# Convolution taps laid between the score groups, and weight splits taken out of the attention, in a two-layer hybrid decoder trunk

## The chip, the cores and the metric

The kernel runs on one core of a Trainium2 chip. The metric is the device time of one execution, in microseconds; lower is better. Three executions of the kernel before took 1790.84, 1791.62 and 1792.38 us, so the median is 1791.62 us. Every change here moves work in time or between engines; what is computed stays the same.

The engines are named as the profile names them: PE is TensorE (PEld its weight loads), DVE is VectorE, ACT is ScalarE, POOL is GpSimd and SP is SyncE, which only issues DMAs here.

## The reference

Two layers run over 512 tokens of width 1024, all in float32:

```python
for l in range(2):
    h = x + 0.5 * swiglu(rms_norm(x), w1, w3, w2)            # FFN 1, inner width 2816
    p = rms_norm(h) @ w_in                                   # 2*384 conv, 384 q, 128 k, 128 v, 256 q_mem
    y_conv = silu(layer_norm(depthwise_conv31(a * sigmoid(gate)) + b))   # 384 channels, causal, 31 taps
    y_swa  = sliding_window_attention(q, k, v, sinks)        # 6 heads of 64, window 128, blocks of 128
    y_mem  = memory_attention(q_mem, mk, mv)                 # 4 heads of 64, 256 memory tokens
    h = h + concat(y_conv, y_swa, y_mem) @ w_out
    h = h + 0.5 * swiglu(rms_norm(h), w1b, w3b, w2b)         # FFN 2
    x = rms_norm(h)
```

Queries and keys are normalised by head and the window's ones rotated. The softmax of the window has a learned sink for each head, whose exponential is added to the denominator.

## The kernel before

**Products.** A float32 product is made of three: each operand is split into a high and a low part (hi is rounded, lo is the rest), and `mm3` (L176 to L178) adds hi·hi, lo·hi and hi·lo. A split is one ACT copy for hi (L145 or L150) and either a DVE subtraction for lo (L146), or, for some weights, a second ACT copy with the sign turned (L151) and an accumulating DMA issued by POOL (L152) that adds the weight to it. Activations are split with their gain by L155 (ACT, `xhi`) and L156 (DVE, `xlo`); L236 squares them for the norm (`sq`). The tiles `whi/wlo` and `ghi/glo` are all such pairs.

**Stages.** In each layer FFN 1 is followed by the mixer (from about 355 to 530 us in layer 0, and some 883 us later in layer 1), the out-projection and FFN 2. The mixer's steps are issued in the order of a string, `ORDER`: `c00` to `c21` are the halves of the convolution's input product for three chunks of 128 channels, `q0` to `q3` the query and key products of four token blocks with the weights wqk (`Q`: their transposes), `v0` to `v3` the value and memory-query products (`V`: transposes), `g0` and `g1` the first two groups of scores, `a` the attention, `t0` to `t2` the convolution's taps, one chunk each, and `s` the layer norm, swish and out-projection. A scheduler then places instructions of all engines by their dependences and its own clock; `tc.issue_after(x)` keeps what stands under it behind the instruction x.

**Attention.** Ten groups of scores (`GROUPS`) go one after another: memory attention (`r`) of blocks 0 and 1, window attention (`w`) of blocks 0, 1, 2, the rest of blocks 1 and 2, then `r` of blocks 2 and 3 and `w` of block 3 in two parts. A group is: scores on PE (L763 with the mask, L769), maxima on DVE (L773 or L788, two reductions), small DVE operations that make the bias (L774, or L789 and L790), the sink's term on POOL (L791, `esw`), exponentials on ACT (L800; `uu`, `pr`), transposes on PE (L810), a copy on ACT (L812, `aux`), and the product with the values on PE (L821, `po`). When a block is complete DVE makes the reciprocal of the denominator (`rd`, L830, L831 or L833) and scales (L835, `aux`), and PE transposes the result (L844, `pt`) for the out-projection. Scores run two groups ahead.

**Taps.** A tap is one DVE instruction over 512 tokens of a chunk of 128 channels (L939, `there`). There are 93 for each layer. The first `EARLY` = 49 may run as soon as their input is there; of the rest, `LATER[n]` are allowed once the bias of group n is made (1, 12, 5, 4, 3, 3, 3, 3, 3, and the last 7 behind the last group), and the scheduler puts them where it finds room, also between the two maxima of a group. When all are done POOL adds the three chunks (L945, L946) for the norm's mean, whose product on PE is L950.

**Splits in the mixer.** wqk has four weight tiles; the last three use the ACT copy and the POOL DMA (`glo<-in_wqk`). The eight weight tiles of the out-projection are split by `out_weights(d)`: d = 0 and 1 after the last key transpose, 2 and 3 inside the attention ahead of groups 3 and 5, the others in `s`. `kept(spread(r), "RL")` copies the layer norm's factor, by ACT. At the end of layer 0 the rescale of h for the next layer (eight DVE operations) runs in one piece inside FFN 1 of layer 1.

Of the kernel before, what the change touches and what calls it, by code (L numbers as in the profile page):

```python
# [13 lines left out]
AF = mybir.ActivationFunctionType  # L14
ALU = mybir.AluOpType
# [49 lines left out]
def trunk(ctx: ExitStack, tc: tile.TileContext, xT, memT, pos, w1a, w3a, w2a, w1b, w3b, w2b,  # L65
# [160 lines left out]
    class Stat:  # L226
# [5 lines left out]
        def square(self, out, src, scale):  # L232
            if self.on:
                self.on.tensor_tensor(out=out, in0=src, in1=src, op=ALU.mult)
            else:
                A.activation(out, src, AF.Square, scale=scale)  # L236

# [103 lines left out]
    def up_pair(l, w13, f, M):  # L341
# [26 lines left out]
        def add(out, a, b):  # L368
            V.tensor_tensor(out=out, in0=a, in1=b, op=ALU.add)  # L369

# [14 lines left out]
        for i in range(2):  # L385
            w = unit(X[i])
            product(xy[i][:, x0], w, 1, 5)
            A.activation(part[i][:, x0], xy[i][:, x0], AF.Copy)
            product(zv[i][:, x1], w, 0, 7)
            add(to[i][:, :, x1], zv[i].rearrange("p (n t) -> p n t", n=2), part[i][:, x0].unsqueeze(1).to_broadcast([P, 2, QT]))  # L390
        w = unit(z)
# [13 lines left out]
    def ffn(l, w13, w2, x, sums, factors, last, at_product, aside=None):  # L405
# [44 lines left out]
        for q, (f0, nf) in enumerate(QUARTERS):  # L450
            ahead = 2 if q + 1 < len(QUARTERS) else 0
            for f in range(f0, f0 + nf + ahead, 2):
                if f not in g:
                    g[f], g[f + 1] = up_pair(l, w13, f, M)
                    if f == PLAIN:
                        with tc.issue_after(M.gated.ins):
                            after()
            begun = []

            def begin(d):  # L460

                w = weights(w2[l, d, :, f0 * P : (f0 + nf) * P], nf * P, V)
                ps = bank([P, S], "mm")
                for j in range(nf - 2):
                    mm3(ps, at(w, ALL, blk(j)), g[f0 + j], j == 0, False)
                begun.append((ps, w))

            for d in range(KD):
                while len(begun) < (d + 1 if ahead or d else 3):
                    with nullcontext() if ahead or d else queued():  # L470
                        begin(len(begun))
                ps, w = begun[d]
                for j in range(nf - 2, nf):
                    mm3(ps, at(w, ALL, blk(j)), g[f0 + j], False, j == nf - 1)
                added = V.scalar_tensor_tensor(out=h[:, d, :], in0=ps, scalar=0.5, in1=h[:, d, :], op0=ALU.mult, op1=ALU.add)  # L475
                if not ahead:
                    last(d)
            if aside and not q:
                aside(added)
# [62 lines left out]
    def heads(x):  # L542
        return x.rearrange("p (h e) -> p h e", e=HD)

    def head_scale(ps, col, n, out=None):

        sq = tm("hsq", "sq", 2)[:, 0 : n * HD]
        A.activation(sq, ps, AF.Square, scale=col)
# [73 lines left out]

    def mixer(l, x, st, last):
        o = CC * TAPS
# [101 lines left out]
        def values(t):  # L726
# [23 lines left out]
        by_half = lambda z: z.rearrange("p (c i) -> p i c", i=2)  # L750
        sinks, nsinks = by_half(sink), by_half(nsink[:, l, :])

        def scored(kind, pairs):
# [17 lines left out]
            if not masked:  # L771
                for i in range(2):
                    V.tensor_reduce(out=nmr[:, b, i], in_=pp[i], axis=AX.X, op=ALU.max)  # L773
                biased[len(biased)] = V.scalar_tensor_tensor(out=nmr[:, b], in0=nmr[:, b], scalar=-1.0, in1=by_half(rm[:, b, :]),  # L774
                                                             op0=ALU.mult, op1=ALU.mult)
                return pp, W
# [5 lines left out]
            else:  # L782
# [3 lines left out]
                rr = by_half(rq[:, b, 0:NH])[:, :, c : c + n]  # L786
            for i in range(2):
                V.tensor_reduce(out=each(nmw, i), in_=pp[i], axis=AX.X, op=ALU.max)  # L788
            V.scalar_tensor_tensor(out=at_(nmw), in0=at_(nmw), scalar=-1.0, in1=rr, op0=ALU.mult, op1=ALU.mult)  # L789
            biased[len(biased)] = V.tensor_tensor(out=at_(nmw), in0=at_(nmw), in1=per(nsinks), op=ALU.min)  # L790
            G.tensor_tensor(out=at_(esw), in0=at_(nmw), in1=per(sinks), op=ALU.add)  # L791
# [31 lines left out]
        def scaled(kind, b, po):  # L823
# [3 lines left out]
            if kind == "w":  # L827
                e = esw[:, b]
                A.activation(e, e, AF.Exp)
                V.tensor_tensor(out=rd.rearrange("p (c i) -> p i c", i=2), in0=po[:, :, HD].rearrange("p (c i) -> p i c", i=2), in1=e, op=ALU.add)  # L830
                V.reciprocal(rd, rd)  # L831
            else:
                V.reciprocal(rd, po[:, :, HD])  # L833
# [27 lines left out]
        def attention():  # L861
# [17 lines left out]

            for d in range(2):  # L880
                with tc.issue_after(keyed[2].ins):
                    out_weights(d)
            yy.extend([gated_pair() for _ in range(KD // 2)][::-1])
            y.extend(at(p, ALL, i, ALL) for p in yy for i in range(2))
            for n, (kind, *pairs) in enumerate(GROUPS):
# [3 lines left out]
                if final:  # L889
# [40 lines left out]

        def taps(c):
            V.tensor_scalar(out=cv[:, c, :], in0=ypad[:, c, 0:S], scalar1=conv_w[:, c, 0:1], scalar2=conv_b[:, c : c + 1],
                            op0=ALU.mult, op1=ALU.add)
            for j in range(1, TAPS):

                n = c * TAPS + j - EARLY
                group = sum(n >= sum(LATER[:g]) for g in range(1, len(LATER)))
                with tc.issue_after(biased[group].ins) if n >= 0 else nullcontext():
                    V.scalar_tensor_tensor(out=cv[:, c, :], in0=ypad[:, c, j : j + S], scalar=conv_w[:, c, j : j + 1],  # L939
                                           in1=cv[:, c, :], op0=ALU.mult, op1=ALU.add)  # L940


        def swish():
# [18 lines left out]
            with queued():  # L962
                RL = kept(spread(r), "RL")
            for c in range(CC):
                s = ring("cv")
                V.tensor_tensor(out=s, in0=cv[:, c, :], in1=RL, op=ALU.mult)
                A.activation(s, s, AF.Silu, scale=ln_g[:, c : c + 1], bias=ln_b[:, c : c + 1])
                split(y[c][0], y[c][1], s, V)
            for d in range(5, KD):
                out_weights(d)  # L970
                out_rows(d, (*MEMORY, *OWN))
# [11 lines left out]
        for i, own in enumerate(ours):  # L983
            raw = wst.tile([P, UNIT], F32, tag="raw", name="raw", bufs=3)
            for j in range(2):
                nc.sync.dma_start(raw[:, blk(j, CCH)], wout[l, 2 * i + j, :, 0:CCH])
            A.activation(own[0], raw[:, 0 : 2 * CCH], AF.Copy)
            A.activation(own[1], raw[:, 0 : 2 * CCH], AF.Copy, scale=-1.0)
            for j in range(2):
# [15 lines left out]
    def stages(st, gain):  # L1005
        def factors(r):
            return gain, kept(spread(r), "R"), lambda: None

        return lambda: rms_cols(st, D), factors

    for l in range(L):
# [15 lines left out]
        before, st = st, Stat("st")  # L1027
        mixer(l, nxt.x, before, into(gn[:, l, N_FFN2], (st, None)))
        sums, factors = stages(st, gn[:, l, N_FFN2])
        st, fin = Stat("st"), gn[:, l, N_FIN]  # L1030
        if l + 1 < L:
# [15 lines left out]
            def factors(r, gg=gg, fin=fin):  # L1047
                R = kept(spread(r[1]), "R")

                def after():  # L1050
                    RF = kept(spread(r[0]), "RL")
# [71 lines left out]
```

## Time and profile before

| | |
|---|---|
| median of three executions | 1791.62 us |
| the profiled execution | 1790.99 us |
| its span | 1789.2 us |
| PE busy | 1757.0 us (98%) |
| DVE busy | 1272.3 us (71%) |
| ACT busy | 899.4 us (50%) |
| POOL busy | 194.4 us (11%) |
| instructions | 28081 |

The span runs from the first to the last instruction, and the profiled execution's own time is 1.8 us longer. A row of time order has its start, its length, engine, line, operation, result and operands with their shapes; in brackets is how long the engine stood idle before it and what released it. A wait row reads: engine, line, what it waited for, total us, how often, the longest. A window row has the stretch and its length, the busy time and instruction count of PE, PEld, DVE, ACT and POOL, then the granted clock of TensorE (1.00 is full), the DMA share and GB/s.

### The profile page before, as it was taken

How to read it: one execution, taken by the hardware profiler on the slowest of the kernel's cores; microseconds unless marked ns; L12 is line 12 of the kernel's file. 1: busy time of each engine (PE TensorE's matmuls, PEld its weight loads, DVE VectorE, ACT ScalarE, POOL GpSimd, SP SyncE). 2: the span in 40 equal slices, each digit the busy share in tenths (PEclk: the TensorE clock that was granted, in tenths of full speed). 3: DMA queues.
4: the chain of work that ended last, by engine and by line, in shares of the span. 5: the costliest groups of instructions: out<-in, count | busy, mean ns of one | idle time of the engine just before them, and what ended most of it. 6: DMA issues, size and time to landing. Idle time of an engine off the chain costs nothing.

```text
span 1789.2 us, 28081 instructions
## 1 busy us (share of the span) xinstructions
PE 1757.0 (98%) x11004; PEld 1581.5 (88%) x11004; DVE 1272.3 (71%) x1887; ACT 899.4 (50%) x1367; POOL 194.4 (11%) x217
## 2 busy tenths in 40 slices
PE   8999999999999999999999999999999999999997
PEld 6989999878788989898889898989787889998986
DVE  6969666589947857575678685756797567666755
ACT  6646444464765535353655453535455655453532
POOL 1001000034221000000010000000441210000000
PEclk9999999999999999999999999999999999999998
DMA  9456555183167547464656474643631966574622
GB/s 280 125 163 177 165 139 145 57 217 70 30 176 172 139 136 177 127 173 128 165 136 170 131 190 135 169 114 105 158 70 30 234 127 171 136 183 119 168 74 82
DMA packets 95892, 253.32 MB, mean 142 GB/s; under 512 B 9872, under 2 KB 14224, under 8 KB 95760
## 3 DMA queue, kind: packets, MB, share of 16 engines
q1 hardware_dynamic: 77040, 190.45, 34.9%
q0 software_dynamic: 18720, 61.09, 19.3%
q8 instruction: 86, 1.41, 0.3%
q14 instruction: 46, 0.38, 0.1%
HBM read 249.40 MB, written 2.10 MB: 141 GB/s over the span
## 4 chain that ended last, share of the span: by engine, by line
PE 81%; issue 6%; DVE 6%; DMA 4%; ACT 3%; POOL 0%; SPq 0%; POOLq 0%; DVEq 0%; ACTq 0%
PE mm L177 12%; PE mm L176 11%; PE mm L178 11%; PE po L176 8%; PE po L178 8%; PE po L177 8%; PE pt L176 6%; PE pt L177 6%; PE pt L178 6%; DVE there L939 2%; DMA glo<-in_wqk 1%; DMA raw<-in_wout 1%; DVE wlo L146 1%; PE cf L178 1%; PE cf L176 1%
## 5 line engine op out<-in xcount | busy, mean ns | idle before, releaser
L145 ACT ACTIVATE whi<-raw 128x1024 fp32r<-128x1024 f32 (+3 forms) x344 | 324.5, 945 | 440.5 <-PE mm L177 223.5
L146 DVE TENSOR_TENSOR wlo<-raw,whi 128x1024 fp32r<-128x1024 f32 (+3 forms) x344 | 372.0, 1083 | 133.9 <-ACT whi L145 132.6
L177 PE MATMUL mm<-glo,whi 128*128 128x512 f32 x752 | 293.3, 390 | 0.8 <-DVE glo L146 0.8
L176 PE MATMUL mm<-ghi,whi 128*128 128x512 f32 x752 | 293.3, 392 | 0.0
L178 PE MATMUL mm<-ghi,wlo 128*128 128x512 f32 x734 | 285.7, 389 | 0.9 <-DVE wlo L146 0.9
L177 PE MATMUL po<-ml,whi 128*128 128x256 f32 x864 | 244.5, 283 | 0.0
L178 PE MATMUL po<-mh,wlo 128*128 128x256 f32 x864 | 244.5, 283 | 0.0
L176 PE MATMUL po<-mh,whi 128*128 128x256 f32 x864 | 244.4, 283 | 0.0
L176 PE MATMUL pt<-xhi,whi 128*128 128x256 f32 x864 | 243.3, 283 | 0.6 <-DVE g L369 0.6
L178 PE MATMUL pt<-xhi,wlo 128*128 128x256 f32 x864 | 243.9, 283 | 0.0
L177 PE MATMUL pt<-xlo,whi 128*128 128x256 f32 x864 | 243.9, 283 | 0.0
L475 DVE SCALAR_TENSOR_TENSOR h<-mm,h 128x512 f32<-128x512 f32 x128 | 87.8, 689 | 133.3 <-PE mm L178 133.3
L177 PEld LDWEIGHTS mm<-glo,whi 128*128 128x128 f32 x752 | 141.3, 188 | 29.9 <-DVE glo L146 1.6
L176 PEld LDWEIGHTS mm<-ghi,whi 128*128 128x128 f32 x752 | 141.3, 188 | 29.4 <-DVE h L475 1.2
L176 PEld LDWEIGHTS pt<-xhi,whi 128*128 128x128 f32 x864 | 165.2, 192 | 1.7 <-DVE g L369 0.8
L177 PEld LDWEIGHTS pt<-xlo,whi 128*128 128x128 f32 x864 | 165.7, 192 | 0.8
L176 PEld LDWEIGHTS po<-mh,whi 128*128 128x128 f32 x864 | 165.8, 192 | 0.7
L177 PEld LDWEIGHTS po<-ml,whi 128*128 128x128 f32 x864 | 165.8, 192 | 0.6
L178 PEld LDWEIGHTS po<-mh,wlo 128*128 128x128 f32 x864 | 165.8, 192 | 0.0
L178 PEld LDWEIGHTS pt<-xhi,wlo 128*128 128x128 f32 x864 | 165.6, 192 | 0.0
L178 PEld LDWEIGHTS mm<-ghi,wlo 128*128 128x128 f32 x734 | 137.8, 188 | 30.2 <-DVE wlo L146 1.3
L939 DVE SCALAR_TENSOR_TENSOR there<-ypad,par,there 128x512 f32<-128x512 f32 x180 | 136.7, 770 | 1.6
(312 smaller groups left out, 3312.9 us busy)
## 6 DMA issues: line engine op xcount, KB each, us to landing
raw<-in_w2a SPq DMA_DIRECT2D x48, 384.0 KB, 3.5
raw<-in_w2b SPq DMA_DIRECT2D x48, 384.0 KB, 3.6
raw<-in_w1b SPq DMA_DIRECT2D x26, 512.0 KB, 3.7
raw<-in_w3b SPq DMA_DIRECT2D x26, 512.0 KB, 4.1
raw<-in_w1a SPq DMA_DIRECT2D x25, 512.0 KB, 3.7
raw<-in_w3a SPq DMA_DIRECT2D x25, 512.0 KB, 3.8
wsum<-in_w1a SPq DMA_DIRECT2D x18, 512.0 KB, 4.5
wsum<-in_w3a SPq DMA_DIRECT2D x18, 512.0 KB, 4.4
```

The source lines that it names most:

```text
L145: A.activation(hi, x, AF.Copy)
L146: on.tensor_tensor(out=lo, in0=x, in1=hi.bitcast(F32), op=ALU.subtract)
L176: T.matmul(ps, a[0], b[0], start=first, stop=False, **more)
L177: T.matmul(ps, a[0], b[1], start=False, stop=False, **more)
L178: tail[0] = T.matmul(ps, a[1], b[0], start=False, stop=last, **more)
L475: added = V.scalar_tensor_tensor(out=h[:, d, :], in0=ps, scalar=0.5, in1=h[:, d, :], op0=ALU.mult, op1=ALU.add)
L939: V.scalar_tensor_tensor(out=cv[:, c, :], in0=ypad[:, c, j : j + S], scalar=conv_w[:, c, j : j + 1], in1=cv[:, c, :], op0=ALU.mult, op1=AL ...
```

## The change

`ORDER` puts V1 behind v2, and g0 and g1 behind V1; between them stands one step `t` that issues the first 55 taps. `LATER` becomes (0, 8, 4, 3, 2, 1, 1, 1, 1, 17): each number of taps is issued behind the bias of its group, and the next group's maxima are kept behind the last of them, so no tap lies between the two maxima. The last taps of chunk 1 take turns with those of chunk 2. Both POOL additions now stand behind the last sink term.

```diff
-ORDER = "c00 c01 q0 c10 q1 c11 Q0 q2 q3 Q1 c20 c21 Q2 v0 v1 V0 Q3 V1 g0 g1 v2 v3 a t0 t1 t2 s"
+ORDER = "c00 c01 q0 c10 q1 c11 Q0 q2 q3 Q1 c20 c21 Q2 v0 v1 V0 Q3 v2 V1 t g0 g1 v3 a s"
-EARLY = 49
-LATER = (1, 12, 5, 4, 3, 3, 3, 3, 3, 3)
+EARLY = 55
+LATER = (0, 8, 4, 3, 2, 1, 1, 1, 1, 17)
...
+        to_do = [(c, j) for c in range(2) for j in range(TAPS)][:EARLY]
+        to_do += [(2, j) for j in range(TAPS - 14)]
+        for j in range(14):
+            to_do += [(1, j) for j in range(j + EARLY - TAPS, TAPS)][:1] if j + EARLY < 2 * TAPS else []
+            to_do.append((2, TAPS - 14 + j))
...
+        def between():
+
+            return tc.issue_after(tapped[-1].ins) if biased else nullcontext()
+
+        def taps_behind(small):
+
+            with tc.issue_after(small.ins):
+                taps(LATER[len(biased)])
+            biased[len(biased)] = small
...
-            for i in range(2):
-                V.tensor_reduce(out=each(nmw, i), in_=pp[i], axis=AX.X, op=ALU.max)
+            with between():
+                for i in range(2):
+                    V.tensor_reduce(out=each(nmw, i), in_=pp[i], axis=AX.X, op=ALU.max)
```

The splits of the out-projection's first four weights move to the value steps. The sink's exponential is kept behind the block's last group of exponentials. The splits of wqk's last three tiles are kept behind the last square of the norm. The last of the weights' own splits goes behind the silus, and RL is copied by DVE.

```diff
+            for d in {0: (0, 1, 2), 2: (3,)}.get(t, ()):
+                with tc.issue_after((squared[-1] if d > 1 else keyed[2]).ins):
+                    out_weights(d)
...
-                A.activation(e, e, AF.Exp)
+                with tc.issue_after(raised[kind, b, CC - 1].ins):
+                    A.activation(e, e, AF.Exp)
...
-            for d in range(2):
-                with tc.issue_after(keyed[2].ins):
-                    out_weights(d)
...
-                if n in (3, 5):
-                    with tc.issue_after(raised[GROUPS[n - 1][0], *GROUPS[n - 1][-1]].ins):
-                        out_weights(len(out_w))
...
-                ww["q"] = [weights(wqk[l, i], 1024, G if i else V, spare()) for i in range(4)]
+                ww["q"] = []
+                for i in range(4):
+
+                    with tc.issue_after(operand.stats[0][0].done.ins) if i else nullcontext():
+                        ww["q"].append(weights(wqk[l, i], 1024, G if i else V, spare()))
...
-                RL = kept(spread(r), "RL")
+                RL = kept(spread(r), "RL", V)
...
+            with tc.issue_after(silus[0].ins) if i == 3 else nullcontext():
+                A.activation(own[0], raw[:, 0 : 2 * CCH], AF.Copy)
+                A.activation(own[1], raw[:, 0 : 2 * CCH], AF.Copy, scale=-1.0)
```

The rescale of h between the layers is cut in halves, one behind the first gated pair and one behind the first products that use the turned sums.

```diff
-                    if f == PLAIN:
-                        with tc.issue_after(M.gated.ins):
-                            after()
+                    if f in (PLAIN, PLAIN + 2):
+                        with tc.issue_after((M.gated if f == PLAIN else M.turned).ins):
+                            after(f > PLAIN)
...
-                    for d in range(KD):
+                    for d in range(4 * half, 4 * half + 4):
```

Three places show what moves. Line numbers of the changed kernel are other ones: L145 to L156 stay, the tap is L778 (before L939), the denominator L873, L874 and L876 (before L830, L831 and L833), the scaling L878 (before L835), the sink's exponential L872 (before L829), exponentials L842 (before L800), the copy L854 (before L812).

DVE at the end of layer 0's attention, from the last group's bias on: before, then the change.

```order
L790 TENSOR_TENSOR nmw<-nmw,nsink 128x2
L939 SCALAR_TENSOR_TENSOR there<-ypad,par,there 128x512
L146 TENSOR_TENSOR glo<-pt,ghi 128x128
L939 SCALAR_TENSOR_TENSOR there<-ypad,par,there 128x512
L833 RECIPROCAL rd_4787<-po 128x4
L939 SCALAR_TENSOR_TENSOR there<-ypad,par,there 128x512
L835 TENSOR_TENSOR aux_3746<-po,rd_4787 128x256
L146 TENSOR_TENSOR glo<-pt,ghi 128x2x128
L939 SCALAR_TENSOR_TENSOR there<-ypad,par,there 128x512 x2
L146 TENSOR_TENSOR glo<-pt,ghi 128x2x128 x2
L939 SCALAR_TENSOR_TENSOR there<-ypad,par,there 128x512 x2
L830 TENSOR_TENSOR rd_4836<-po,esw 128x2x3
```

```order
L778 SCALAR_TENSOR_TENSOR there<-ypad,par,there 128x512 x4
L146 TENSOR_TENSOR glo<-pt,ghi 128x128
L876 RECIPROCAL rd_4880<-po 128x4
L778 SCALAR_TENSOR_TENSOR there<-ypad,par,there 128x512 x2
L878 TENSOR_TENSOR aux_3746<-po,rd_4880 128x256
L146 TENSOR_TENSOR glo<-pt,ghi 128x2x128
L778 SCALAR_TENSOR_TENSOR there<-ypad,par,there 128x512
L146 TENSOR_TENSOR glo<-pt,ghi 128x2x128
L778 SCALAR_TENSOR_TENSOR there<-ypad,par,there 128x512 x2
L146 TENSOR_TENSOR glo<-pt,ghi 128x2x128
L778 SCALAR_TENSOR_TENSOR there<-ypad,par,there 128x512 x7
L873 TENSOR_TENSOR rd_4929<-po,esw 128x2x3
```

Seven taps stand between the last bias and the last block's denominator `rd` before, 16 after; a 17th follows it, ahead of the reciprocal.

ACT in the middle of the attention, at the first window group's exponentials (`esw` is the sink's term, whi and wlo an out-projection weight).

```order
L800 ACTIVATE pr<-mm,nmw,rq 128x128 x2
L829 ACTIVATE esw<-esw 128x6
L800 ACTIVATE uu<-mm,nmw,rq 128x128 x2
L150 ACTIVATE whi<-raw 128x640
L812 ACTIVATE aux_3745<-pt 128x512
L151 ACTIVATE wlo<-raw 128x640
L812 ACTIVATE aux_3745<-pt 128x2x128
```

```order
L842 ACTIVATE pr<-mm,nmw,rq 128x128 x2
L842 ACTIVATE uu<-mm,nmw,rq 128x128 x2
L872 ACTIVATE esw<-esw 128x6
L854 ACTIVATE aux_3745<-pt 128x512
L854 ACTIVATE aux_3745<-pt 128x2x128
```

The sink's exponential has gone behind the last pair of exponentials, and the weight's two copies are no longer there.

POOL at the beginning of layer 0's mixer: the three accumulating DMAs of wqk, the norm's inverse root `rsq`, and the next DMAs.

```order
L152 DMA glo<-in_wqk 128x1024 x3
L193 TENSOR_TENSOR rsq_3796<-ms_3794,nhalf 128x4
L152 DMA wlo<-in_wconv 128x1024 x3
L706 TENSOR_TENSOR uu<-query,sg 128x6x32 x2
L706 TENSOR_TENSOR uu<-query,sg 128x2x32 x2
```

```order
L152 DMA glo<-in_wqk 128x1024
L193 TENSOR_TENSOR rsq_3796<-ms_3794,nhalf 128x4
L152 DMA glo<-in_wqk 128x1024 x2
L152 DMA wlo<-in_wconv 128x1024 x3
L713 TENSOR_TENSOR uu<-query,sg 128x6x32 x2
```

The inverse root now stands ahead of the second and third DMA.

More of the change, by code (lines that the diff above doesn't have):

```diff
@@ L621, in prepare, with mixer @@
         memory(l)
[L623 removed]
+    def mixer(l, operand, st, last):
+        x = operand.x
         o = CC * TAPS
@@ L751, in mixer, with taps @@
         sinks, nsinks = by_half(sink), by_half(nsink[:, l, :])
+        to_do = [(c, j) for c in range(2) for j in range(TAPS)][:EARLY]
[3 more added lines that the diff above has]
+            to_do.append((2, TAPS - 14 + j))
+        tapped = []
+        def taps(n=EARLY):
+            for c, j in [to_do.pop(0) for _ in range(n)]:
+                if not j:
+                    t = V.tensor_scalar(out=cv[:, c, :], in0=ypad[:, c, 0:S], scalar1=conv_w[:, c, 0:1], scalar2=conv_b[:, c : c + 1],
+                                        op0=ALU.mult, op1=ALU.add)
+                else:
+                    t = V.scalar_tensor_tensor(out=cv[:, c, :], in0=ypad[:, c, j : j + S], scalar=conv_w[:, c, j : j + 1],
+                                               in1=cv[:, c, :], op0=ALU.mult, op1=ALU.add)
+                tapped.append(t)
+        def between():
[4 more added lines that the diff above has]
+            biased[len(biased)] = small
         def scored(kind, pairs):
@@ L786, in scored @@
                 rr = by_half(rq[:, b, 0:NH])[:, :, c : c + n]
-            for i in range(2):
-                V.tensor_reduce(out=each(nmw, i), in_=pp[i], axis=AX.X, op=ALU.max)
+            with between():
+                for i in range(2):
+                    V.tensor_reduce(out=each(nmw, i), in_=pp[i], axis=AX.X, op=ALU.max)
             V.scalar_tensor_tensor(out=at_(nmw), in0=at_(nmw), scalar=-1.0, in1=rr, op0=ALU.mult, op1=ALU.mult)
-            biased[len(biased)] = V.tensor_tensor(out=at_(nmw), in0=at_(nmw), in1=per(nsinks), op=ALU.min)
+            small = V.tensor_tensor(out=at_(nmw), in0=at_(nmw), in1=per(nsinks), op=ALU.min)
+            taps_behind(small)
             G.tensor_tensor(out=at_(esw), in0=at_(nmw), in1=per(sinks), op=ALU.add)
@@ L928, in out_rows @@
                     mm3(oo[d], at(out_w[d], ALL, blk(n)), y[CC + n], n == CC, False)
[L931 to L940, printed above, removed]
+        silus = []
         def swish():
@@ L1006, in factors @@
         def factors(r):
-            return gain, kept(spread(r), "R"), lambda: None
+            return gain, kept(spread(r), "R"), lambda half: None
         return lambda: rms_cols(st, D), factors
```

30 lines of the change are left out of this document (16 added, 14 removed).

## The prediction

> **What bounds the kernel now.** I read the page first (span, engines, chain), then the windows by stage, the waits of TensorE inside the two mixers, the order in time around its longest wait, and last the DMA queues where the weight splits move.
>
> ```profile
> span 1789.2 us, 28081 instructions
> PE 1757.0 (98%) x11004; PEld 1581.5 (88%) x11004; DVE 1272.3 (71%) x1887; ACT 899.4 (50%) x1367; POOL 194.4 (11%) x217
> PE 81%; issue 6%; DVE 6%; DMA 4%; ACT 3%; POOL 0%; SPq 0%; POOLq 0%; DVEq 0%; ACTq 0%
> ```
>
> TensorE is busy for 1757.0 of 1789.2 us. The change adds and removes no product, so it can only win back part of the 32.2 us in which TensorE stands, and any time in which it runs at a lower clock. Where those are, by stage of layer 0 (the last row is the attention of layer 1):
>
> ```profile
> 340.00:376.00 36.00, 35.26 (x183) 29.46 (x182) 26.84 (x40) 24.77 (x37) 1.72 (x2) 1.00 0.50 144
> 376.00:437.00 61.00, 60.83 (x293) 51.68 (x293) 53.92 (x90) 24.77 (x40) 28.25 (x29) 1.00 0.61 142
> 437.00:500.00 63.00, 57.86 (x416) 49.15 (x414) 55.05 (x119) 40.69 (x95) 12.47 (x13) 0.97 0.13 25
> 1320.00:1384.00 64.00, 59.00 (x412) 50.48 (x413) 55.09 (x119) 40.44 (x94) 12.49 (x13) 0.95 0.12 24
> ```
>
> The columns are busy time of PE, PEld, DVE, ACT and POOL, then granted clock, DMA share and GB/s. The attention loses 5.14 us (63 minus 57.86) in layer 0 and 5.00 in layer 1, and both show a clock under 1.00. DVE is busy for 55 of 63 us there, so it is nearly as full as TensorE. The waits by name, of the attention and then of the end of the convolution's first product:
>
> ```profile
> PE po L821 <- ACT aux L812: 1.8, 1, 1.8
> PE pt L810 <- ACT aux L812: 1.7, 3, 0.7
> PE pt L581 <- ACT there L583: 0.8, 1, 0.8
> PE pt L810 <- DVE glo L146: 0.8, 1, 0.8
> ...
> PE mm L176 <- ACT xhi L155: 0.5, 1, 0.5
> PE mm L177 <- DVE xlo L156: 0.3, 1, 0.3
> ```
>
> **The attention's middle.** The longest wait of TensorE, 1.83 us, in time order:
>
> ```profile
> 454.73 1.27 POOL L945 TENSOR_TENSOR aux<-there 128x512 f32<-128x512 f32 x1
> 455.96 0.65 POOL L791 TENSOR_TENSOR esw<-nmw,rw 128x6 f32<-128x6 f32 x1
> 456.64 0.21 ACT L829 ACTIVATE esw<-esw 128x6 f32<-128x6 f32 x1 [0.94 <-POOL esw L791]
> 457.44 0.73 ACT L150 ACTIVATE whi<-raw 128x640 fp32r<-128x640 f32 x1
> 458.07 0.59 ACT L812 ACTIVATE aux<-pt 128x512 f32<-128x512 f32 x1
> 458.71 1.11 PE L821 MATMUL po<-mvn,aux 128*128 128x65 f32 x8 [1.83 <-ACT aux L812]
> ...
> 460.00:464.00 4.00, 4.00 (x21) 2.53 (x19) 3.04 (x6) 1.93 (x6) 0.91 (x2) 0.59 0.86 153
> 1342.00:1348.00 6.00, 6.00 (x26) 4.53 (x26) 3.29 (x7) 2.68 (x7) 1.49 (x2) 0.50 0.60 109
> ```
>
> POOL's sum of convolution chunks (L945) keeps esw back; ACT waits 0.94 for it with the exponential of esw (L829), then runs a weight split (0.73 for whi) before the copy that TensorE needs. The change takes out all three: the sum on POOL moves behind the last group, the exponential moves behind the last one of its block, the splits leave the attention. So 1.83 goes, and the 0.7 wait of the same kind (longest of the second waits row). V1's turn behind v2 removes 0.8 (third row). Behind the 1.83 wait the granted clock is 0.59 over 4 us in layer 0 and 0.50 over 6 in layer 1. Full compensation would be 4 × 0.41 = 1.6 and 6 × 0.50 = 3.0 us; TensorE does not run back to back there, so I take 1.4 and 3.0. That they go with the wait is an inference: the dip follows the wait within 4 us in both layers.
>
> [...] The trace has the dip in both layers behind this wait and behind no shorter one, and I go by the trace.
>
> What the reorder adds here: six more taps stand ahead of group 0's maxima (55 for 49).
>
> ```profile
> 429.08 3.39 DVE L939 SCALAR_TENSOR_TENSOR there<-ypad,par,there 128x512 f32<-128x512 f32 x5
> 443.19 3.90 DVE L939 SCALAR_TENSOR_TENSOR there<-ypad,par,there 128x512 f32<-128x512 f32 x5
> 442.51 1.93 ACT L800 ACTIVATE uu<-mm,nmr,rm 128x256 f32<-128x256 f32 x4
> 448.79 0.60 PE L810 MATMUL pt<-cst,uu 128*128 128x128 f32 x4
> ```
>
> A tap costs 3.39/5 = 0.68 us where two chains alternate and 3.90/5 = 0.78 in one chain; I take 0.70 for the mixture. Six are 4.2 us. The first four exponentials ended at 444.44 and TensorE came for them at 448.79, a slack of 4.35. With TensorE 0.8 earlier it waits 4.2 + 0.8 − 4.35 = 0.7 us. Bounds: 0 if DVE starts its taps early enough, 1.9 if all are priced at 0.78 and the cover v3 (issued between) slips. Gain of the middle: 0.8 + 1.8 + 0.7 + 1.4 − 0.7 = 4.0 us in layer 0, 5.6 in layer 1 (3.0 for the clock). No group's maxima are parted by a tap any more; since the wait for scores, not DVE, then sets the pace, I give nothing more for that.
>
> **The attention's end.** The last group's final small operation, the last taps, and what they hold up, before:
>
> ```profile
> 486.70 0.16 DVE L790 TENSOR_TENSOR nmw<-nmw,nsink 128x2 f32<-128x2 f32 x1
> 491.87 1.53 DVE L939 SCALAR_TENSOR_TENSOR there<-ypad,par,there 128x512 f32<-128x512 f32 x2
> 495.55 0.17 DVE L830 TENSOR_TENSOR rd<-po,esw 128x6 f32<-128x6 f32 x1 [2.16 <-PE po L821]
> 495.98 0.56 DVE L835 TENSOR_TENSOR aux<-po,rd 128x384 f32<-128x384 f32 x1
> 496.73 0.49 PE L844 MATMUL pt<-cst,aux 128*128 128x128 f32 x3
> ```
>
> Seven taps follow the last group before, 17 after; in the changed order rd (L830) of the last block stands behind 16 of them, its reciprocal behind all 17. Ten more taps are 7.0 us (6.8 to 7.8). DVE stood 2.16 us ahead of rd, which they fill. The rest, 4.84, lengthens the way from the last small operation to the transposes L844. That operation cannot come earlier than TensorE's scores allow, so by the middle's gain: 4.0 and 5.6. L844 thus moves by 7.0 − 2.16 − 4.0 = +0.8 us in layer 0 and −0.8 in layer 1; with taps at the low end and no wait at the first exponentials −0.1 and −1.7, and another 1.2 better if none of TensorE's copies waits anywhere (−1.3, −2.9). The short waits of the tail (the rest of the second row, and 0.8 for glo) lie ahead of L844 and give nothing, since DVE is the later one. What TensorE does after L844 is the same in both orders. The two sums on POOL start when their taps are done; the products between L844 and the norm's own product, the same ones in both orders, cover them.
>
> **The wqk splits.** ACT ran ghi/glo between the last xhi; now all three pairs follow the last square.
>
> ```profile
> 373.12 0.70 ACT L155 ACTIVATE xhi<-h,gn 128x512 fp32r<-128x512 f32 x1
> 374.26 1.04 ACT L150 ACTIVATE ghi<-raw 128x1024 fp32r<-128x1024 f32 x1
> 370.45 0.86 POOL L152 DMA_DIRECT2D glo<-in_wqk  x1 [32.45 <-ACT glo L151]
> 376.54 0.86 POOL L152 DMA_DIRECT2D glo<-in_wqk  x1 [2.16 <-ACT glo L151]
> 377.10 2.23 POOL L193 TENSOR_TENSOR rsq<-ms,nhalf 128x4 f32<-128x4 f32 x1
> 387.28 0.50 PE L177 MATMUL mm<-glo,xhi 128*128 128x512 f32 x1 [0.17 <-DMA glo<-in_wqk]
> DMA to landing us min/median/max: 8.5/9.4/10.7
> 370.42 0.68 DVE L475 SCALAR_TENSOR_TENSOR h<-mm,h 128x512 f32<-128x512 f32 x1
> ```
>
> The last h is there at 371.10, so xhi runs there, not at 373.12, and the waits of 0.5 and 0.3 go (the rows quoted first), some 0.9 us with what they drag. But the first glo ends after xhi, square and a pair of splits: 371.1 + 0.7 + 0.6 + 1.0 + 0.9 = 374.3 (an estimate, the square like an xhi without its addition), so its DMA issues 3.9 us later. The second waits on POOL behind rsq, 2.23 us, which now lies between; the third issues at about 378.5, 2.0 later. Before, the third landing already was late by 0.17 at 387.28. The end of this query product moves by −0.9 if the landings are hidden, +2.0 if the last keeps its 10.7 us, +3.9 if the three queue up behind the first one's delay. The raw tiles come free later too, so fewer transfers share the engines with the last one; I take +1.0 in each layer, and keep −0.9 and +3.9. All of it reaches the attention, for v2 and the scores follow on TensorE without slack (0.17 us idle in 61).
>
> [...]
>
> **Small parts.**
>
> ```profile
> PE mm L177 <- DVE glo L146: 0.3, 1, 0.3
> PE mm L178 <- DVE wlo L146: 0.9, 1, 0.9
> ```
>
> RL's copy on DVE instead of ACT shortens the way to the glo on which the out-projection waits (0.3 in layer 0, first row; I take the same for layer 1): −0.6. The rescale of h in two halves lets the wlo split between: −0.9, once. The four early out-weight splits run beside V products, where ACT is busy 24.77 of 61 us; the last own split behind the silus is the reverse, later, but its rows are the last that the projection needs. Both cost nothing while that cover stands.
>
> **Sum.** +0.8 − 0.8 (attention) + 2 × 1.0 (wqk) − 0.6 − 0.9 = +0.5 us against the profiled execution's 1790.99 (span 1789.2 and 1.8 around it), 1791.5. The median shown, 1791.62, is 0.6 above that execution, so about 1792 as a median. What can be told from no change is 0.2%, 3.6 us.
>
> **Rivals.**
> - *The wait moves to the end and takes the clock along* (slower). TensorE's waits ahead of L844 grow by 4.84 to some 6.6 us with those already there. The place is the last block's rd behind 16 taps; it decides from a wait of about 1.8 us in one piece, after which the clock fell before. Price: the same dip in the out-projection, 1.4 to 3.0 per layer, 4.4 together: 1796.4. For it: the dips behind 1.83. Against: three shorter waits of 0.5 to 0.8 there cost no clock before, and the wait may fall in pieces. [...]
> - *The glo landings queue* (slower): +3.9 instead of +1.0 in each layer, 5.8 more: 1797.8. For it, landings that grew from 8.5 to 10.7; against, one of 2.0 us later issue.
> - *The middle's gain is kept* (faster): landings hidden (−0.9 twice), attention at its best (−1.3 and −2.9), small parts −1.5: −7.5, 1784.1. For it, 5 us of wait per attention and a DVE with 8 us idle in 63; against, the tail's 17 taps.
>
> **Chances.** The forecast (a shift, within 0.2%) 0.37; the gain kept 0.31; the wait and clock at the end 0.22; the landings 0.10. So faster 0.31, same 0.37, slower 0.32. The range takes in the ends of the sum, 1784 and 1798, with 1 us for the median: 1783 to 1799. The likeliest case's own range is 1788 to 1795.
>
> **What would show it.** In the changed profile: no wait over 1 us of the products po in the middle and a clock of 1.00 there; DVE idle for scores before the last group; a wait of several us at the last two transposes of the block outputs, released by DVE's aux; glo of wqk named as a releaser of TensorE with 1 to 2 us. Wrong if the tail waits under 3 us (then faster), or if the granted clock falls in the out-projection (then slower).

## The result and the profile after

The changed kernel takes 1801.64 us (median of four executions, 1799.65 to 1804.6) against 1791.23 of the kernel before in the same comparison. The ratio is 1.0059, 95% interval 1.0042 to 1.0077: slower by 0.6%. The forecast was 1792, range 1783 to 1799. The profiled execution of the changed kernel took 1802.96 us, its span is 1801.2.

The page of the changed kernel, its windows over layer 0's mixer, and the head of the list of TensorE's waits over the whole span (total, times, longest):

```profile
span 1801.2 us, 28081 instructions
PE 1762.9 (98%) x11004; PEld 1584.9 (88%) x11004; DVE 1275.5 (71%) x1889; ACT 899.1 (50%) x1365; POOL 191.9 (11%) x217
...
376.00:437.00 61.00, 57.93 (x265) 48.01 (x264) 50.06 (x83) 26.53 (x39) 26.55 (x29) 0.97 0.58 141
437.00:500.00 63.00, 59.18 (x418) 51.35 (x418) 56.63 (x119) 41.17 (x96) 12.50 (x13) 0.95 0.18 36
...
PE mm L177 <- DMA glo<-in_wqk: 7.6, 5, 2.2
PE mm L176 <- ACT xhi L155: 6.3, 2, 6.1
PE pt L887 <- DVE aux L878: 2.9, 2, 1.7
PE mm L808 <- ACT there L585: 2.9, 2, 1.4
PE pt L887 <- DVE glo L146: 2.5, 2, 1.3
```

The 1.83 us waits of the product `po` are gone from the list. In their place stand 7.6 us for glo of wqk, 2.9 + 2.5 us at the block outputs' transposes (L887, before L844), and 2.9 us for V1's copy. The stretch 376 to 437, which lost 0.17 us before, now loses 3.07.

To place the loss I compare the starts of the same TensorE rows in both traces: the norm's column sums (N), the first product of c10, which follows q0 (Q), the first mask product of the window's scores (G0), the last mask product of the last group (G9), the last block's transposes (T), the convolution norm's product (P), its column sums (C), and the next norm's column sums (X). Each entry is the length of a stretch in the kernel before, and what the changed kernel adds to it, in us:

| stretch | layer 0 | layer 1 |
|---|---|---|
| N to Q, the query product | 13.30, +4.48 | 13.55, +4.68 |
| Q to G0 | 60.57, +0.69 | 60.58, +0.65 |
| G0 to G9, the middle | 34.54, −3.54 | 36.22, −5.21 |
| G9 to T, the end | 13.05, +4.95 | 13.07, +4.94 |
| T to P | 3.79, 0.00 | 3.76, +0.04 |
| C to X, the out-projection | 38.77, +1.48 | 38.94, +2.00 |

N itself is 0.60 us earlier in layer 0, where the waits for xhi and xlo are gone. From X of layer 0 to N of layer 1 the changed kernel wins 2.50 us. All of it together gives the 12.0 us by which the spans differ; the medians differ by 10.4.

The three DMAs of wqk and the query product that waits for them, changed kernel, in time order:

```profile
374.96 0.86 POOL L152 DMA_DIRECT2D glo<-in_wqk  x1 [36.58 <-ACT glo L151]
377.07 0.90 POOL L152 DMA_DIRECT2D glo<-in_wqk  x1
378.75 0.87 POOL L152 DMA_DIRECT2D glo<-in_wqk  x1 [0.78 <-ACT glo L151]
387.40 0.79 PE L177 MATMUL mm<-glo,xhi 128*128 128x512 f32 x1 [2.22 <-DMA glo<-in_wqk]
391.18 0.50 PE L177 MATMUL mm<-glo,xhi 128*128 128x512 f32 x1 [0.85 <-DMA glo<-in_wqk]
```

The first was issued at 370.45 before, 4.5 us earlier; the third at 376.54, 2.2 earlier. The second and third landings stand 3.8 us apart, and TensorE goes on after the third at 391.18 instead of 387.28. From issue to landing the three took 8.5, 9.4 and 10.7 us before and 7.1, 10.3 and 12.4 now, so the landings move by 3.1, 4.4 and 3.9 us.

The end of the attention, DVE's rows from the last bias on, the transposes, and the clock there (4 us windows):

```profile
487.09 0.16 DVE L831 TENSOR_TENSOR nmw<-nmw,nsink 128x2 f32<-128x2 f32 x1
494.73 6.36 DVE L778 SCALAR_TENSOR_TENSOR there<-ypad,par,there 128x512 f32<-128x512 f32 x7
501.01 0.16 DVE L873 TENSOR_TENSOR rd<-po,esw 128x6 f32<-128x6 f32 x1
502.01 0.56 DVE L878 TENSOR_TENSOR aux<-po,rd 128x384 f32<-128x384 f32 x1
502.71 0.52 PE L887 MATMUL pt<-cst,aux 128*128 128x128 f32 x3 [1.22 <-DVE aux L878]
...
493.00:497.00 4.00, 3.80 (x15) 3.61 (x16) 3.96 (x6) 0.67 (x2) 1.27 (x1) 0.50 0.02 4
497.00:501.00 4.00, 4.00 (x17) 3.45 (x17) 3.82 (x6) 0.00 (x0) 0.00 (x0) 0.65 0.00 0
```

`rd` no longer waits for TensorE (2.16 us before): it waits behind the taps, and TensorE waits for it. From last bias to transposes it took 10.0 us before and takes 15.6 now. The wait reads as 1.22 because TensorE ran its last products ahead of it at a clock of 0.50 and 0.65: in g1 below, with a clock of 1.00 from 493 to 501, the same wait reads 4.18, and G9 to T is as long.

### The profile page after: what moved, and what is told of

It is laid out like the page before. It is cut to its first block, busy times and chain, and to the rows that moved or that the text cites. A ratio compares the mean times of both kernels' runs of the same rounds, so it can differ in the third digit from the quotient of the medians.

```text
span 1801.2 us, 28081 instructions
## 1 busy us (share of the span) xinstructions
PE 1762.9 (98%) x11004; PEld 1584.9 (88%) x11004; DVE 1275.5 (71%) x1889; ACT 899.1 (50%) x1365; POOL 191.9 (11%) x217
## 4 chain that ended last, share of the span: by engine, by line
PE 85%; issue 6%; DMA 4%; DVE 3%; ACT 2%; SPq 0%; POOL 0%; POOLq 0%; DVEq 0%; ACTq 0%
PE mm L177 12%; PE mm L176 12%; PE mm L178 12%; PE po L176 9%; PE po L178 9%; PE po L177 9%; PE pt L176 6%; PE pt L177 6%; PE pt L178 6%; DMA glo<-in_wqk 1%; DVE there L778 1%; PE po L863 1%; PE mm L808 1%; DMA raw<-in_w1b 1%; PE cf L176 1%
## 5 line engine op out<-in xcount | busy, mean ns | idle before, releaser
L145 ACT ACTIVATE whi<-raw 128x1024 fp32r<-128x1024 f32 (+3 forms) x344 | 324.4, 945 | 451.2 <-PE mm L177 227.5
L778 DVE SCALAR_TENSOR_TENSOR there<-ypad,par,there 128x512 f32<-128x512 f32 x180 | 136.0, 770 | 2.1
```

Of the source, the lines that this page charges most:

```text
L145: A.activation(hi, x, AF.Copy)
L778: t = V.scalar_tensor_tensor(out=cv[:, c, :], in0=ypad[:, c, j : j + S], scalar=conv_w[:, c, j : j + 1], in1=cv[:, c, :], op0=ALU.mult, op ...
```

## The experiments

Ratios are against the kernel before, run on the same chip as each experiment. Each experiment also left one trace, from which the stretches come; g1, a single execution, is not in the table.

| kernel | median us | ratio, 95% interval |
|---|---|---|
| changed kernel | 1801.64 | 1.0059, 1.0042 to 1.0077 |
| e1, wqk order undone | 1792.95 | 1.0016, 1.0006 to 1.0025 |
| e2, seven taps at the end | 1795.85 | 1.0032, 1.0022 to 1.0043 |
| e3, last own split undone | 1803.42 | 1.0074, 1.0059 to 1.0089 |
| e4, all three undone | 1788.39 | 0.9988, 0.9978 to 0.9998 |
| f1, wqk order alone | 1799.06 | 1.0039, 1.0026 to 1.0052 |
| f2, e2 with two glo on DVE | 1784.34 | 0.9957, 0.9942 to 0.9972 |
| f3, e4 with a split moved | 1787.55 | 0.9976, 0.9967 to 0.9986 |
| f5, POOL's sum late, alone | 1790.64 | 0.9993, 0.9983 to 1.0003 |
| g2, f2 with the own split undone | 1784.64 | 0.9967, 0.9954 to 0.9980 |
| g3, 17 taps at the end, alone | 1794.90 | 1.0028, 1.0016 to 1.0039 |
| g4, g2 with a split moved | 1784.44 | 0.9969, 0.9958 to 0.9980 |

**e1, the wqk order undone.**

```diff
-                    with tc.issue_after(operand.stats[0][0].done.ins) if i else nullcontext():
+                    with nullcontext():
```

> The changed kernel with one part undone: the splits of wqk's last three tiles may run between the last xhi again. Theory A (three separate losses: late glo of wqk, 17 taps at the end of the attention, out-projection): TensorE lost 2.2 + 0.9 us on the late glo in layer 0 and 0.2 + 2.2 + 2.1 in layer 1, with a clock dip behind, some 4.4 and 4.7 us between its norm transposes and the end of q0, against 0.6 to 0.9 won before it; undone, 7 to 8 us come back, about 1794. Theory B (only the end of the attention bounds; lateness ahead of it is absorbed by idle time of VectorE): at most 2 us, about 1800.

The ratio falls by 0.43% against the changed kernel's, some 7.7 us. N to Q is +1.14 and −0.01 against the kernel before instead of +4.48 and +4.68. Of the waits for glo 0.4 us is left, in layer 1, as in the kernel before; the +1.14 goes with a clock of 0.50 from 378 to 380 in this trace, of which the last section says more. Theory A's size; theory B, in which idle time of VectorE takes up the lateness, falls.

**f1, the wqk order alone,** in the kernel before: the same constraint added, nothing else.

> The kernel before with one part of the change alone: the splits of wqk's last three tiles behind the last square. Theory A (the late landings move everything behind them): TensorE waits 3 to 4.5 us for glo in each layer, the end of q0 moves by 3.8, and all of it reaches the end: 6 to 8 us slower than the kernel before. Rival (VectorE is the bound in the attention of the kernel before and takes up the lateness): the end of q0 moves by 3.8 too, but the attention's end by less than 2, at most 3 us slower.

7.0 us slower (0.39%). N to Q grows by 5.33 and 3.64, and G9 to T is unchanged (0.00 and −0.02), so VectorE does not take the lateness up there, and the 7.0 us are the size of theory A. In layer 1 of this trace the middle is 1.63 shorter, which is the clock's doing (last section). The waits of TensorE from 376 to 437 in it hold one line; the clock is 0.50 from 388 to 394, which makes up the rest of the 5.33:

```profile
PE mm L177 <- DMA glo<-in_wqk: 3.0, 2, 2.0
```

**f2, what in the wqk order is late.** To e2 (next) it adds that DVE's subtraction makes two of the three glo:

```diff
-                        ww["q"].append(weights(wqk[l, i], 1024, G if i else V, spare()))
+                        ww["q"].append(weights(wqk[l, i], 1024, G if i == 1 else V, spare()))
```

> The changed kernel with seven taps at the end (as in e2) and with two of the three late glo made by VectorE's subtraction instead of ScalarE's copy and the accumulating DMA; the late order on ScalarE stays. Theory A1 (the DMA landings are what is late): no wait for glo in q0 is left, the end of q0 stands 0.6 to 0.9 us ahead of the kernel before, 8 to 9 us faster than e2, 1787 to 1788. Theory A2 (ScalarE's late copies are the cause): the wait for glo stays, released by VectorE, 1 to 3 us in each layer, and the gain on e2 is under 4 us.

No wait for glo is left in either query product, N to Q is −0.43 and −0.71, and the kernel is 0.43% faster than the one before. Theory A1: ScalarE's order was not what cost, the DMAs queued behind it were. The step from e2 (0.75% by the two ratios, 13 us, uncertain by some 3) is larger than the 8 to 9 expected. The two traced executions differ by 10.8: 4.8 and 4.4 are in N to Q, and 1.2 in where N of layer 0 starts.

**e2, seven taps at the end.**

```diff
-LATER = (0, 8, 4, 3, 2, 1, 1, 1, 1, 17)
+LATER = (0, 8, 5, 4, 4, 3, 3, 2, 2, 7)
```

> The changed kernel with LATER = (0, 8, 5, 4, 4, 3, 3, 2, 2, 7): seven taps behind the last group as in the kernel before, ten more between the earlier groups. Theory A: the wait at the last block's transposes (about 5.2 us in each layer more than before, with its clock dip) goes, and part of it comes back as later maxima in the middle, where VectorE had some 6 us idle: 4 to 9 us faster, 1793 to 1797. Theory B: all of the loss is here, 10 us, about 1791. If VectorE were the bound throughout, the ten taps cost the same anywhere: no change, 1801.

The ratio falls by 0.27%, 4.8 us. G9 to T is −0.71 in both layers instead of +4.95, and the middle keeps −0.95 and −2.64 of its −3.54 and −5.21: of 5.66 us won at the end 2.6 are paid for in the middle. Clock and waits of its attention (layer 0, then 1):

```profile
437.00:500.00 63.00, 58.06 (x426) 50.02 (x425) 57.78 (x126) 41.55 (x97) 14.56 (x15) 1.00 0.19 39
1320.00:1384.00 64.00, 59.06 (x433) 50.80 (x432) 58.20 (x126) 41.55 (x97) 14.71 (x15) 1.00 0.19 38
```

TensorE still stands 4.9 us in each, in pieces of 0.8 at most but for V1's 1.4, and the clock is 1.00 throughout.

**g3, 17 taps at the end alone,** in the kernel before, placed by the scheduler.

```diff
-LATER = (1, 12, 5, 4, 3, 3, 3, 3, 3, 3)
+LATER = (1, 12, 5, 3, 2, 1, 1, 1, 1, 17)
```

> The kernel before with LATER = (1, 12, 5, 3, 2, 1, 1, 1, 1, 17) alone: ten taps moved from the middle groups behind the last group, but left to the scheduler there, so that rd of the last block stands behind 11 of them and not 16. Theory P (what costs is rd's place behind the taps): from group 9's scores to the last block's transposes 1.5 to 3 us more than before instead of 4.9, then up to 2 us more at the norm's product, which waits for the last tap. Theory N (the number alone counts): 4.9 us as in the change. In both the middle gains 1 to 3 us in each layer; in all 1 to 6 us slower.

G9 to T grows by 0.48 and 0.46 only, although as many taps follow the last group as in the change: the scheduler put `rd` behind 10 of them and its reciprocal behind 11, where the change has 16 and 17. T to P grows by 1.61 and 1.65, for the norm's product now waits for the last tap and POOL's sum:

```profile
499.85 0.52 PE L844 MATMUL pt<-cst,aux 128*128 128x128 f32 x3 [0.93 <-DVE aux L835]
505.25 1.12 PE L950 MATMUL pt<-aux,onesq 128*128 128x512 f32 x2 [1.43 <-POOL aux L946]
```

So the place of `rd` counts (theory P), with even less than expected. The middle was expected to win 1 to 3; it lost 1.47 in layer 0 and won 1.67 in layer 1, with the 1.8 us waits still in it, and both sizes are those of the clock behind them (last section). In all 4.9 us slower.

**f5, the cause of the 1.83 us wait alone:** POOL's first sum is kept behind the last sink term.

```diff
+        sunk = []
...
-            G.tensor_tensor(out=at_(esw), in0=at_(nmw), in1=per(sinks), op=ALU.add)
+            sunk.append(G.tensor_tensor(out=at_(esw), in0=at_(nmw), in1=per(sinks), op=ALU.add))
...
-            G.tensor_tensor(out=s1, in0=cv[:, 0, :], in1=cv[:, 1, :], op=ALU.add)
+            with tc.issue_after(sunk[-1].ins):
+                G.tensor_tensor(out=s1, in0=cv[:, 0, :], in1=cv[:, 1, :], op=ALU.add)
```

> The kernel before with one cause of its 1.83 us wait removed: POOL's sum of the first two convolution chunks is kept behind the last sink term; splits and taps stay. The prediction's chain (sum, sink term, its exponential, split, copy): 0.94 us of ScalarE's wait go, the 1.83 us wait falls to about 0.9, and with it the clock dip if it hangs on the wait: 0.9 + 1.4 and 0.9 + 3.0, some 6 us faster at most if nothing is lost at the end, about 2 if the dip stays. Rival: VectorE is full there and gives the time back at the end of the attention: under 1 us.

The chain holds: the wait at that product falls to 0.8, and the middle is 2.11 and 3.78 us shorter, near the 2.3 and 3.9 that wait and dip were priced at together. But G9 to T grows by 2.58 and 2.54, and the time does not change. The waits of TensorE in the middle (450 to 480) and at the end (480 to 502), the clock at the end, and the sum on POOL with the tap beside it (the lines are two and more further on than in the kernel before):

```profile
PE pt L812 <- ACT aux L814: 1.1, 2, 0.8
PE po L823 <- ACT aux L814: 0.8, 1, 0.8
...
PE pt L812 <- DVE glo L146: 1.3, 1, 1.3
PE pt L812 <- ACT aux L814: 1.0, 2, 0.6
PE pt L846 <- DVE glo L146: 0.2, 1, 0.2
...
492.00:494.00 2.00, 1.72 (x12) 1.73 (x13) 1.96 (x4) 0.60 (x1) 0.00 (x0) 0.77 0.03 8
494.00:496.00 2.00, 2.00 (x7) 1.61 (x7) 0.00 (x0) 0.00 (x0) 1.27 (x1) 0.50 0.00 0
...
487.18 1.26 POOL L948 TENSOR_TENSOR aux<-there 128x512 f32<-128x512 f32 x1
487.27 1.72 DVE L941 SCALAR_TENSOR_TENSOR there<-ypad,par,there 128x512 f32<-128x512 f32 x1
```

The wait and the dip moved to the end together. That is the rival of the prediction, seen here without the change's taps. What the sum took along shows in the last two rows: the tap that starts just behind it takes 1.72 us, the others there 0.75. In the kernel before the long tap (1.47) stood beside the sum in the middle, at 455.08. Here it stands ahead of the glo that TensorE waits for at the end, and that wait grows from 0.79 to 1.34. That the sum is what stretches the tap fits all these traces, but no run takes the sum away.

**e3 and e4.** In e3 the last own split is as before:

```diff
-            with tc.issue_after(silus[0].ins) if i == 3 else nullcontext():
+            with nullcontext():
```

> The changed kernel with one part undone: the last of the out-projection's own splits no longer waits for the silus. Theory A: its raw buffer is held until the silus end, so the next FFN's weights arrive late, ScalarE stands 6 us waiting for w1b ahead of the silus, and TensorE waits for glo twice; undone, 1.5 us in layer 0 and 2.0 in layer 1 come back, about 1798. Theory B: covered, no change, 1801.

It is not faster, where theory A expected some 3.5 us: 1.0074, its interval overlaps the changed kernel's. In its trace C to X is −0.19 and +0.71, so the place looks better, but the glo waits and T to P of that trace are longer. Theory A's third loss falls as a cause in the time.

> The changed kernel with all three of these undone; what stays of the change: V1 and g0, g1 later, no tap between a group's maxima, out-weight splits and POOL sums out of the attention, RL on VectorE, h in halves. Theory A: the three add up, 13 to 20 us faster than the changed kernel, 1782 to 1788, so 3 to 9 faster than the kernel before. Theory B: as with seven taps at the end alone, about 1791.

e4 holds the undoings of e1, e2 and e3: 12.7 us less than the changed kernel by the ratios, where e1 and e2 give 7.7 + 4.8 = 12.5. The two losses add up, within intervals that leave some 4 us open, and the third adds nothing, so that e4 ends at the low edge of the 13 to 20 expected. What is left of the change wins 0.12% on the kernel before.

**f3, V1's copy.** In e4 the fourth out-projection split moves one value step ahead:

```diff
-            for d in {0: (0, 1, 2), 2: (3,)}.get(t, ()):
+            for d in {0: (0, 1), 1: (2, 3)}.get(t, ()):
```

> The version with all three undone (e4), and the fourth out-projection split moved from the third value step to the second, so that it no longer stands ahead of V1's copy on ScalarE. Expected if that split makes the 1.43 us wait for V1's copy ahead of group 0's scores: the wait falls to 0 to 0.8 us in each layer, 1.2 to 2.8 us faster than e4. Rival: the wait is set by v2 and V1 themselves, or what is won there is waited for again at group 0's exponentials: no change against e4.

The cause is right: in layer 0 the wait for V1's copy falls from 1.4 to 0.2 and Q to G0 from +0.69 to +0.01. The middle then is 1.0 us longer in both layers than in e4, so nothing is won in the attention. The ratio is 0.0012 lower, 2 us, with intervals that overlap and no place for it in the stretches.

**g1, the changed kernel again,** one execution and one trace.

> The changed kernel once more, for what its traces repeat. Theory A (losses in the place and of the size seen): waits for glo in q0 of 3 to 4.5 us in each layer, the last block's transposes 4.9 us later against group 9's scores than in the kernel before. Not expected to repeat, if they are chance landings of DMAs: the 1.5 and 2.0 us lost between the convolution's norm and the next norm, since kernels that differ from it only ahead of that place lost 0 to 0.4 there.

It took 1808.59 us. N to Q (+4.52, +4.28), the middle (−3.52, −5.21) and the end (+4.98, +4.94) repeat to 0.4 us or better. C to X is +0.17 and +2.30: layer 0's loss there did not repeat, layer 1's did. New are Q to G0 in layer 1, +2.28 for +0.65, with a clock of 0.50 from 1284 to 1286, and T to P, +1.28 and +1.64, where the trace above had 0.00 and +0.04. From X to layer 1's N it loses 0.6 where the first trace won 2.5.

**g2 and g4, the best version.**

> The version of f2 (seven taps at the end, two of the three glo made by VectorE), with the last own split no longer behind the silus. If that split costs nothing under the cover there: as f2, 0.995 to 0.997 of the kernel before, 1783 to 1786. If it costs: 1 to 3 us faster than f2.

> As g2_best, with the fourth out-projection split at the second value step (as in f3). In f3 the 0.7 us won at V1's copy was waited for again in the middle: no change against g2 if that holds here; 1 to 2 us faster if it does not.

Both are within f2's interval. The last own split costs nothing there, and the fourth split is worth nothing. f2, at 1784.34 us and 0.43% faster than the kernel before (g2 and g4 say 0.3%), is as good as any: the change with seven taps at the end and two glo on DVE.

## Why the prediction was wrong

The forecast summed to +0.5 us; the spans differ by 12.0. By its own terms:

- **The wqk splits, forecast +1.0 in each layer.** Measured at Q: 4.48 − 0.60 = +3.9 in layer 0, and in layer 1 4.68 less the 1.0 of xhi and xlo waits that are gone, +3.7. This is the step that failed most, 5.6 us in all. The end of the range, +3.9, was right and I called it a rival with a chance of 0.10. Wrong was the reason for +1.0, that fewer transfers would share the engines: the loads of wconv's raw tiles start later too (374.69 to 381.15 for 370.59 to 378.48), and the DMA share in the changed kernel stays at 1.00 to 1.07 from 376 to 400. Three landings behind a first that was issued 4.5 us late moved as a whole, by 3.1, 4.4 and 3.9 us. f1 shows that this part alone costs 7.0 us, and f2 that it is the landings.
- **V1's copy, a gain of 0.8 in each layer.** It became a loss of 0.7. I priced the four moved splits at nothing because ScalarE is idle for half of that stretch, and did not look where in ScalarE's order they stand. The fourth stands ahead of V1's copy:

```profile
446.32 0.74 ACT L150 ACTIVATE whi<-raw 128x640 fp32r<-128x640 f32 x1
446.95 0.74 ACT L151 ACTIVATE wlo<-raw 128x640 fp32r<-128x640 f32 x1
447.57 0.39 ACT L585 ACTIVATE there<-pt 128x256 f32<-128x256 f32 x1
448.02 0.48 PE L808 MATMUL mm<-mT,there 64*128 64x256 f32 x1 [1.43 <-ACT there L585]
```

  f3 takes it away and gives nothing in the attention: the size of this error is real, its worth is not.
- **The middle without V1, forecast 3.2 and 4.8.** Measured 3.54 and 5.21: near, but not term by term. From G0 to G9 TensorE's idle time falls from 2.54 to 0.21 us in layer 0 (2.3 for the 2.5 forecast), and its busy time by 1.21, in layer 1 by 2.90, the clock's part (1.4 and 3.0 forecast). The wait of 0.7 at the first exponentials, which was set against these, did not come. That the dip goes with the 1.83 us wait is no longer only an inference: it stands behind that wait in both layers of all three kernels that have it (before, f1, g3), and there is none in the middle of any other. That layer 1 gains more was luck, for it is not always layer 1 that has the long dip (last section).
- **The end, forecast 7.0 − 2.16 = 4.84.** G9 to T grew by 4.95 and 4.94, and the cause is right, `rd` behind 16 taps (e2 and g3). The forecast was for another stretch, from the last bias to the transposes, and that grew by 5.6; the last bias came 0.65 sooner after G9, so part of the agreement is luck. The ten taps took 7.8 us, the upper bound, and not 7.0. Of that, 0.9 is one tap: it starts just behind POOL's first sum (494.55 to 495.82) and takes 1.64 us, the six after it 0.75 each. The sum's new place, in the middle of the taps that keep `rd` back, was priced at nothing. Q to T together came out at +2.1 and +0.4 where +0.8 and −0.8 were forecast; V1 is most of the difference.
- **The clock at the end,** the slower rival. It came, at 0.50 and 0.65, but fell ahead of T, where TensorE had to wait for DVE anyway, and cost nothing more (T to P 0.00 and +0.04). In g1 it fell later, behind waits for `rd` of 4.18 and 2.69, and T to P grew by 1.28 and 1.64; in e3 by 1.32 in layer 0. So the place was right, and the price 0 to 1.6, not 1.4 to 3.0.
- **The small parts, −1.5.** The wait of 0.9 for wlo is gone from the list. In the out-projection −0.3 for each layer was forecast and +1.48 and +2.00 measured. TensorE's waits for ghi and glo there rose from 0.28 and 0.48 to 0.99 and 1.65, about half of it, so RL's copy on DVE did not take the wait for glo away. I blamed the last own split, and e3, g2 and the kernels with that split late and no such loss (e1: −0.54, −0.02) speak against it. What costs there stays open: it is 0.2 to 2.3 in two traces of the same kernel. I had not reckoned with traces that differ that much; four times of the changed kernel spread over 5 us. Four of the kernel before spread over 2, but the 17 to 25 that the experiments were compared with spread over 5 to 6 too.

The misses sum up to 5.6 (wqk) + 2.5 (attention) + 4.1 (out-projection, with RL) − 0.6 (between the layers) = 11.6, which is the 12.0 less the 0.5 forecast. The range ended at 1799 because each of its ends stood alone: the wqk end and the loss behind the attention were not added.

## What to carry to other kernels

Where transfers queue on a busy DMA (its share was 1.00 to 1.07 here), do not price a late issue by the last one's delay but look at the first one's: here the third landing came 3.9 us later, near the first issue's delay of 4.5 and not its own of 2.2. When an engine is said to have room for a moved instruction, read what stands right behind it in that engine's order, and who waits for that. Filler work for an idle gap belongs behind the last operation that another engine waits for, not merely behind the last group: here the same 17 taps cost 4.9 us with `rd` behind 16 of them, and 0.5 plus 1.6 when `rd` could pass some. And moving one instruction off a critical stretch can move what runs slowly beside it: a long tap went along with POOL's sum, 1.72 us in f5 and 1.64 in the change, where the others took 0.75.

## What the runs showed of the hardware

The length of one wait did not decide whether the clock fell. In f5 it went to 0.50 at the end with no wait over 1.3 us; in e2 it stayed at 1.00 in both mixers, behind waits for glo of up to 2.2 and one of 1.4 for V1's copy. In e1, f3 and f5 it was 0.50 from 378 to 380 behind waits for xhi and xlo of 0.4 to 0.5 and 0.3; the kernel before has the same two waits (0.5 and 0.3) and 1.00 there. Behind the 2.2 us wait for glo the clock was 0.90 and 0.68 in the changed kernel's first trace (384 to 392), and 1.00 in the second, where the wait is 2.3 (the second row is the first trace's):

```profile
388.00:392.00 4.00, 1.88 (x9) 1.22 (x8) 3.76 (x5) 2.16 (x3) 0.86 (x1) 1.00 1.03 283
388.00:392.00 4.00, 3.15 (x10) 2.00 (x9) 3.60 (x5) 2.31 (x3) 0.95 (x2) 0.68 1.04 308
```

Nor is a dip always as long. The kernel before, f1 and g3 all have the 1.83 us wait in both layers. The middle takes 34.5 to 34.6 us in four of these six mixers, and 36.0 and 36.2 in the other two: layer 0 of g3 and layer 1 of the kernel before. The clock was at 0.50 for about twice as long there: in the kernel before from 1342 to 1348 in layer 1, and from 461 to 464 in layer 0. So 1.5 to 1.7 us of a stretch can come and go with the wait as it was, and the 1.63 of f1, the 1.47 and 1.67 of g3 and the forecast's larger gain in layer 1 are of this kind.

What decides whether the clock falls behind a wait, and for how long, no run here shows. The waits right ahead of the dips were 1.83 us in the kernel before and 1.3 in f5. Longer ones, the 4.18 of g1, had a dip behind them too (0.66 from 501 to 505):

```profile
502.94 0.87 PE L887 MATMUL pt<-cst,aux 128*128 128x128 f32 x3 [4.18 <-DVE aux L878]
```
